# Hybrid decoder layer: 128-byte tiles, query and key norms by 1024 tokens, second half first, memory's part in the middle, state halves swapped by copies

## The chip, the core and the metric

The kernel runs on one core of one Trainium2 chip, as one program. The metric is device microseconds of one execution. Engines are named as the profile names them: PE (TensorE, matmul), DVE (VectorE), ACT (ScalarE), POOL (GpSimd) and SP, whose queue issues all the DMAs here. Each engine runs its own instructions strictly in the order in which the built program holds them.

## The reference

One decoder layer on x of 2048 tokens by 1024 features, all in float32:

```
hn   = rms_norm(x, norm_mix);  proj = hn @ w_in          # q, k, v (512 each), 8 gate logits, u (512)
q, k = rms_norm over each head's 64 columns              # 8 heads
fox  = softmax(q k^T / 8 + c_q - c_k, causal) v          # c = cumsum(log_sigmoid(gate logit))
y    = S5(u): 32 groups of 16 channels, each one complex diagonal state of 64; gelu, then glu
h    = x + [rms_norm(fox), rms_norm(y)] @ w_out
h    = h + cross_attention(rms_norm(h), rms_norm(mem)) @ w_xo     # 256 memory tokens, 4 heads of 256
h    = h + (silu(conv3(gate)) * up) @ w_ffn_down                  # d_ff = 2816
```

Only the first of these stages is touched by the change beyond tile addresses: the input projection, the S5 scan that runs beside it, and the projection of the memory tokens to keys and values.

## The kernel before, in words

Every float32 matmul is made of three (`mm3`, lines 65 to 67), with each operand split into a high and a low part: ACT writes the high part, DVE subtracts it from the source to get the low part (`split`, lines 71 and 72; `split_scaled`, lines 77 and 78, does it with a gain). So each loaded tile costs one pass on ACT and one on DVE.

The stages run one after the other: A (input projection, S5, memory's keys and values), then the causal attention, C (output projection and cross-attention), D and E (the MLP). Stage A ends where the first attention scores (`sps`) begin. It has these parts, in the order of the program:

- The u columns for four chunks of 512 tokens (tile `pps`). Each chunk loads and splits 8 tiles of x and takes the sum of squares of its tokens. When the chunk with c = 2 is on, `mem_norm` (line 289) loads, splits and sums the memory tokens.
- `mem_part` (line 290): 8 blocks of weights for the memory's keys and values (tiles `xkp`, `xvp`). Its first two blocks also reload chunks 0 and 1 of x, because SBUF holds two chunks at a time.
- Twelve units (lines 335 to 361). A unit is one half of the tokens (1024) times one 256-column block of the weights: blocks 0 and 1 are q, 2 and 3 are k, 4 and 5 are v. Each has 192 matmuls of 256 columns. Half 0 comes first, as [2, 0, 1, 3, 4, 5], then half 1 as [4, 0, 2, 1, 3, 5]. Before half 1, `ahead` loads and splits chunks 2 and 3 again, 16 tiles. After the first v block of half 1, `forget` turns the gate logits into the cumulative sums on DVE.

A q or k unit works in four steps of 256 tokens. `qk_begin` (line 307) does 48 matmuls into a PSUM bank (`qps`, four banks in turn), squares it on ACT (`qsq`), sums per head on DVE (`qss`, 8 columns), makes the inverse root with `rinv` (lines 89 to 95: DVE, two ACT instructions, three DVE instructions, all on 8 columns), and multiplies the bank by it on DVE (`qf`). `qk_end` (line 324) comes one step later: PE transposes `qf` (tile `qst`), ACT and DVE split it (`qy`), and two DMAs store it.

The S5 scan is a generator that the stage advances in small steps (`go`, line 229) between its own instructions. After a set-up it handles 16 batches of two groups. For each batch POOL builds rotation tables `er`, `ei` and weights with 12 instructions (`s5_tables`, line 569), and `s5_main` (line 648) does, on a tile whose partitions 0 to 63 hold real parts and 64 to 127 imaginary parts: matmuls to `z`; a rotation, which needs each half multiplied into the other half's place (lines 669 to 672); two scans along time (line 675); a rotation back (lines 681 to 684), of which POOL does one half (line 682); a split; and matmuls to `yp`.

Names that the steps below touch: `et` and `rt` (norms per token), `whl` and `wraw` (weights split and raw), `ul`, `xl`, `tl`, `cl`, `bl` (low parts), `ks`, `bp` (S5 set-up per batch), `gates` and `fsc` (forget).

Of the kernel before, what the change touches and what calls it, by code (L numbers as in the profile page):

```python
# [8 lines left out]
F32 = mybir.dt.float32  # L9
# [14 lines left out]
HD = 64  # L24
# [13 lines left out]
MAGIC = 12582912.0  # L38
TP1 = 6.28125
# [125 lines left out]
def consts(ctx, K, pk):  # L165
# [4 lines left out]
    cp = ctx.enter_context(tc.tile_pool(name="const", bufs=1, reuse_waits="tile"))  # L170
# [37 lines left out]
def stage_a(ctx, K, xT, win, wf, memT, wxk, wxv, qD, kD, vD, uD, cD, xkD, xvD, side):  # L208
# [16 lines left out]
    mp = (tp, wp, xr, xtile, psm, pss)  # L225
# [12 lines left out]
    rp = early.enter_context(tc.tile_pool(name="ar", bufs=1, side="right", reuse_waits="tile"))  # L238
# [33 lines left out]
    for c in range(NC):  # L272
# [19 lines left out]
    def v_unit(half, j, w):  # L292
        for t in range(8 * half, 8 * half + 8):
# [13 lines left out]
    def qk_begin(p, j, w, g, dst):

        ps = psm.tile([128, 2, 256], F32, tag="mm", name="qps")
        for i in range(2):  # L310
            c, o = p // 2, (2 * p + i) % 4 * 128
            for k in range(KT):
                mm3(nc, ps[:, i], x[c][k][0][:, o : o + 128], x[c][k][1][:, o : o + 128], w[0][:, k], w[1][:, k], k == 0, k == KT - 1)
        heads = lambda q: q.rearrange("p i (h d) -> p (i h) d", d=HD)
        sq = tp.tile([128, 2, 256], F32, tag="tm", name="qsq")
        nc.scalar.activation(sq, ps, AF.Square)
        ss = tp.tile([128, 8], F32, tag="ss", name="qss")
        nc.vector.reduce_sum(out=ss, in_=heads(sq), axis=AX.X)
# [3 lines left out]
        return f, p, j, g, dst  # L322

    def qk_end(f, p, j, g, dst):

        st = pss.tile([128, 2, 256], F32, tag="st", name="qst")
        for a in range(2):
            for i in range(2):
                nc.tensor.transpose(st[:, a, i * 128 : (i + 1) * 128], f[:, i, a * 128 : (a + 1) * 128], K.ident)
# [15 lines left out]
    for i, (half, tix) in enumerate(units):  # L345
# [3 lines left out]
        else:  # L349
            for p in range(4 * half, 4 * half + 4):  # L350
                new = qk_begin(p, tix % 2, w, *((K.g_q, qD) if tix < 2 else (K.g_k, kD)))
                if late:
                    qk_end(*late)
# [1476 lines left out]
```

## Time and profile before

| what | value |
|---|---|
| median of 3 runs | 3213.03 us (3209.97 to 3213.67) |
| the profiled execution's own time | 3209.64 us |
| its span, first to last instruction | 3207.7 us |
| mean granted TensorE clock | 0.966 |
| PE busy, share of the span | 94% |
| DVE busy, share of the span | 67% |

The profile describes one execution, whose own time is 1.9 us more than its span. A share of the whole span is a mean over stages that are limited by different things. Stage A takes the first 622 us. "Granted clock" is the mean over a stretch of the TensorE clock, where 1.00 is 2.4 GHz and 0.50 is 1.2 GHz.

### The profile page before, as it was taken

The numbers are of one execution on the slowest core, as the hardware profiler recorded it, in microseconds if no ns is written. First come the engines' busy times: TensorE is split into PE (matmuls) and PEld (weight loads), VectorE is DVE, ScalarE is ACT, GpSimd is POOL, SyncE is SP. The second block draws the span as 40 slices with busy tenths as digits, with TensorE's granted clock in tenths as the row PEclk, the third lists the DMA queues.
The fourth block names the chain that finished last, engine by engine and source line by source line (L and its number), as shares of the span: only waits on it lengthen the run. The fifth ranks groups of instructions, "written<-read, shape, count | busy, mean of one in ns | idle before, by whom it ended". The sixth has DMA issues, their size and how long they took to land.

```text
span 3207.7 us, 43620 instructions
## 1 busy us (share of the span) xinstructions
PE 3012.0 (94%) x15532; PEld 2536.3 (79%) x15532; DVE 2148.2 (67%) x3472; ACT 1451.9 (45%) x2644; POOL 851.9 (27%) x820
## 2 busy tenths in 40 slices
PE   7898978999999899999999697999999999999999
PEld 6687868888888677888878476788788887888887
DVE  8868899688887866444543787777977776443332
ACT  5443333488887634344531343444544444333221
POOL 3615674010000431000000356444444443000000
PEclk9898988999999899999999798999999999999999
DMA  6863434555443663311353335222422222664542
GB/s 194 155 192 107 150 113 127 167 152 151 128 128 114 191 180 128 116 60 63 96 167 126 104 125 179 93 79 86 145 84 81 86 85 103 220 207 157 178 157 84
DMA packets 297649, 421.83 MB, mean 132 GB/s; under 512 B 96341, under 2 KB 168789, under 8 KB 296281
## 3 DMA queue, kind: packets, MB, share of 16 engines
q1 hardware_dynamic: 297432, 419.06, 41.9%
q8 instruction: 122, 2.00, 0.3%
q14 instruction: 95, 0.77, 0.1%
HBM read 304.04 MB, written 114.93 MB: 131 GB/s over the span
## 4 chain that ended last, share of the span: by engine, by line
PE 70%; DVE 12%; DMA 6%; issue 4%; POOL 4%; ACT 3%; SPq 1%; POOLq 0%; DVEq 0%; ACTq 0%
PE da L1567 9%; PE de L1567 6%; PE dps L66 5%; PE dps L67 5%; PE dps L65 5%; PE cmm L65 4%; PE cmm L66 4%; PE cmm L67 4%; PE pt L824 3%; PE dd L1567 3%; PE db L1567 3%; PE sps L790 2%; PE po L817 2%; PE po L818 2%; PE sps L791 2%
## 5 line engine op out<-in xcount | busy, mean ns | idle before, releaser
L1567 PE MATMUL da<-xf,wf 128*128 128x512 f32 x1584 | 380.4, 393 | 19.9 <-ACT xf L71 9.8
L1567 PEld LDWEIGHTS da<-xf,wf 128*128 128x128 f32 x1584 | 299.1, 189 | 86.2 <-ACT xf L71 11.7
L71 ACT CAST whl<-wraw 128x1024 fp32r<-128x1024 f32 (+2 forms) x132 | 155.7, 1203 | 357.8 <-PE dps L67 285.8
L65 PE MATMUL cmm<-act,whl 128*128 128x512 f32 x760 | 308.4, 406 | 2.1 <-DVE h L1220 1.2
L1419 POOL TENSOR_TENSOR wsum<-wraw 128x512 f32<-128x512 f32 x88 | 119.5, 1360 | 717.7 <-DVE h L1391 499.8
L66 PE MATMUL cmm<-act,whl 128*128 128x512 f32 x760 | 302.6, 398 | 3.7 <-DVE act L72 3.7
L67 PE MATMUL cmm<-act,whl 128*128 128x512 f32 x760 | 301.5, 397 | 0.0
L1567 PE MATMUL de<-xf,wf 128*128 128x512 f32 x1056 | 268.9, 405 | 33.2 <-ACT kp L1571 29.1
L65 PE MATMUL dps<-hf,whl 128*128 128x512 f32 x704 | 275.2, 391 | 4.4 <-DVE whl L72 4.4
L66 PE MATMUL dps<-hf,whl 128*128 128x512 f32 x704 | 275.1, 391 | 2.4 <-DVE hf L72 2.4
L67 PE MATMUL dps<-hf,whl 128*128 128x512 f32 x704 | 274.8, 390 | 0.0
L1567 PEld LDWEIGHTS de<-xf,wf 128*128 128x128 f32 x1056 | 206.2, 196 | 83.1 <-ACT kp L1571 32.5
L72 DVE TENSOR_TENSOR whl<-wraw,whl 128x1024 fp32r<-128x1024 f32 (+2 forms) x132 | 190.7, 1466 | 52.2 <-ACT whl L71 51.9
L814 DVE TENSOR_TENSOR pl<-pt,ph 128x512 fp32r<-128x512 f32 (+1 forms) x320 | 186.7, 605 | 22.1 <-ACT ph L828 20.5
L1689 DVE TENSOR_TENSOR res<-dps,res 128x512 f32<-128x512 f32 x32 | 22.1, 691 | 267.0 <-PE dps L67 267.0
L72 DVE TENSOR_TENSOR wf<-wsum,wf 128x512 fp32r<-128x512 f32 x176 | 165.4, 941 | 44.0 <-ACT wf L71 43.5
L66 PEld LDWEIGHTS cmm<-act,whl 128*128 128x128 f32 x760 | 144.9, 191 | 40.6 <-DVE act L72 6.5
L824 PE MATMUL pt<-pk,sb 128*128 128x128 f32 x1088 | 173.1, 276 | 3.9 <-DVE pl L814 2.7
L828 ACT CAST ph<-pt 128x512 fp32r<-128x512 f32 (+1 forms) x320 | 158.9, 521 | 39.0 <-PE pt L824 36.5
L65 PEld LDWEIGHTS cmm<-act,whl 128*128 128x128 f32 x760 | 144.7, 190 | 38.7 <-issue 2.4
L67 PEld LDWEIGHTS cmm<-act,whl 128*128 128x128 f32 x760 | 144.3, 190 | 32.6
L799 ACT ACTIVATE sb<-sb,m 128x128 f32<-128x128 f32 (+15 forms) x128 | 154.6, 1208 | 23.0 <-DVE m L795 22.8
(477 smaller groups left out, 7745.6 us busy)
## 6 DMA issues: line engine op xcount, KB each, us to landing
wraw<-wup SPq DMA_DIRECT2D x88, 512.0 KB
wraw<-wdn SPq DMA_DIRECT2D x64, 704.0 KB
hD<-gt SPq DMA_DIRECT2D x88, 256.0 KB
hraw<-hD SPq DMA_DIRECT2D x88, 256.0 KB
qhl<-qD SPq DMA_DIRECT2D x128, 128.0 KB
wraw<-win SPq DMA_DIRECT2D x28, 512.0 KB
x<-xT SPq DMA_DIRECT2D x32, 256.0 KB
xr<-xT SPq DMA_DIRECT2D x32, 256.0 KB
```

Source lines behind the costliest of these rows:

```text
L65: nc.tensor.matmul(out, lhsT=al, rhs=bh, start=first, stop=False)
L66: nc.tensor.matmul(out, lhsT=ah, rhs=bl, start=False, stop=False)
L67: nc.tensor.matmul(out, lhsT=ah, rhs=bh, start=False, stop=last)
L71: nc.scalar.copy(hi, src)
L72: (eng or nc.vector).tensor_tensor(lo, src, hi.bitcast(F32), op=ALU.subtract)
L790: nc.tensor.matmul(out, lhsT=ql[:, o : o + 128], rhs=kc, start=True, stop=False)
L799: nc.scalar.activation(sb[:, :wid], sb[:, :wid], AF.Exp, bias=m, scale=-1.0, accum_out=self.ls[:, i : i + 1])
L814: v.tensor_tensor(b, c, a.bitcast(F32), op=ALU.subtract)
L824: nc.tensor.transpose(ps[:, j * 128 : (j + 1) * 128], rows[j][:, kt * 128 : (kt + 1) * 128], K.ident)
L828: nc.scalar.copy(ph[:, s], ps[:, s])
L1419: gp.tensor_tensor(t, x, y, op=op)
L1567: nc.tensor.matmul(ps, lhsT=w[:, a, k], rhs=x[k][:, b], start=first and k + j == 0, stop=k == 3 and j == 2, skip_group_check=not first)
```

## The change

- All SBUF pools go through `Rounded`, which pads a tile's free size to a multiple of 128 bytes, and a 96-byte tile at the right edge moves the pools there to such multiples. The eight gain columns become slices of one tile `gains`.
- The memory's part (`mem_norm`, `mem_part`) moves from ahead of the twelve units to between the sixth and the seventh.
- The units of half 1 come first. Chunks 2 and 3 are still in SBUF then, so their reload goes; chunks 0 and 1 are reloaded in `mem_part` as before.
- A q or k unit copies each step's PSUM bank to SBUF on ACT (`qf`, 8 buffers in a pool of their own). The sums of squares of all four steps go into one tile of 32 columns, `norms` makes one `rinv` for them, in the next unit, and multiplies the four `qf` tiles in place. The transposes (`end`) follow after that.
- In `s5_main`, ACT copies the two halves of `z` and of the scan's result `w3` crosswise into a tile `cross`, and the rotations become DVE instructions on all 128 partitions. POOL's half of the rotation back goes to DVE. Signs move from one sum to the other.

```diff
+class Rounded:
+    def tile(self, shape, dtype, **kw):
+        unit = 64 if dtype == BF16 else 32
+        n = math.prod(shape[1:])
+        if n % unit == 0:
+            return self.pool.tile(shape, dtype, **kw)
+        t = self.pool.tile([shape[0], -(-n // unit) * unit], dtype, **kw)[:, :n]
...
-        if c + 2 == NC:
-            mem = mem_norm(K, mp, memT)
-    mem_part(K, mp, mem, wxk, wxv, xkD, xvD, lambda c: load(c, xr, "xr", 4), go)
...
-        r = rinv(K, tp, ss, 8, 1.0 / HD, et[:, 2 * p : 2 * p + 2].rearrange("p i h -> p (i h)"), tag="rsm")
-        f = tp.tile([128, 2, 256], F32, tag="qf", name="qf", bufs=3)
-        nc.vector.tensor_tensor(heads(f), heads(ps), r.unsqueeze(2).broadcast_to([128, 8, HD]), op=ALU.mult)
...
+        def begin(self, n):
...
+            f = fp.tile([128, 2, 256], F32, tag="qf", name="qf")
+            nc.scalar.copy(f, ps)
+            sq = tp.tile([128, 2, 256], F32, tag="tm", name="qsq")
+            nc.scalar.activation(sq, ps, AF.Square)
+            nc.vector.reduce_sum(out=self.ss[:, n], in_=sq.rearrange("p i (h d) -> p (i h) d", d=HD), axis=AX.X)
+            self.f.append(f)
+
+        def norms(self):
+            e = et[:, 8 * self.half : 8 * self.half + 8].rearrange("p i h -> p (i h)")
+            r = rinv(K, tp, self.ss.rearrange("p n h -> p (n h)"), 32, 1.0 / HD, e, tag="rsm")
+            for n, f in enumerate(self.f):
+                q = f.rearrange("p i (h d) -> p (i h) d", d=HD)
+                nc.vector.tensor_tensor(q, q, r[:, 8 * n : 8 * n + 8].unsqueeze(2).broadcast_to([128, 8, HD]), op=ALU.mult)
...
-    units = [(half, tix) for half in range(2) for tix in ([4,0,2,1,3,5] if half else [2,0,1,3,4,5])]
-
-    def ahead(i):
-        if i == 6:
-            for c in (2 * units[i][0], 2 * units[i][0] + 1):
-                load(c, xr, "xr", 4)
-        return weights(units[i][1])
...
+    units = [(half, tix) for half in (1, 0) for tix in ([4, 0, 2, 1, 3, 5] if half == 0 else [2, 0, 1, 3, 4, 5])]
...
+        if i == 5:
+            mem = mem_norm(K, mp, memT)
...
+            new = QK(half, tix % 2, w, *((K.g_q, qD) if tix < 2 else (K.g_k, kD)))
+            for n in range(4):
+                new.begin(n)
+                if n == 0 and late:
+                    late.norms()
+                if n > 0:
+                    end(n - 1)
                 go(1.3)
...
+        if i == 5:
+            mem_part(K, mp, mem, wxk, wxv, xkD, xvD, lambda c: load(c, xr, "xr", 4), go)
...
+    def crossed(src):
+        t = sp.tile([128, n, 256], F32, tag="cr", name="cross")
+        nc.scalar.copy(t[0:64], src[64:128])
+        nc.scalar.copy(t[64:128], src[0:64])
+        return t
+
+    zc = crossed(z)
     v.tensor_tensor(w1, z, er, op=ALU.mult)
-    v.tensor_tensor(w2[0:64], z[64:128], ei[64:128], op=ALU.mult)
-    v.tensor_tensor(w2[64:128], z[0:64], ei[0:64], op=ALU.mult)
-    v.tensor_tensor(w1, w1, w2, op=ALU.add)
+    v.tensor_tensor(w2, zc, ei, op=ALU.mult)
+    v.tensor_tensor(w1, w1, w2, op=ALU.subtract)
...
-    gp.tensor_tensor(x2[0:64, :, a], w3[64:128, :, p], ei[64:128, :, p], op=ALU.mult)
-    v.tensor_tensor(x2[64:128, :, a], w3[0:64, :, p], ei[0:64, :, p], op=ALU.mult)
-    v.tensor_tensor(x1[:, :, a], x1[:, :, a], x2[:, :, a], op=ALU.subtract)
+    v.tensor_tensor(x2[:, :, a], wc[:, :, p], ei[:, :, p], op=ALU.mult)
+    v.tensor_tensor(x1[:, :, a], x1[:, :, a], x2[:, :, a], op=ALU.add)
```

The built program's order shows the change at three places. Line numbers of before and of the change differ for the same text: `rinv` is at L89 to L95 before and at L115 to L121 now, `split` at L71 and L72 before and at L97 and L98 now.

On DVE, one step of the first k unit before (`qss` is the sum of squares per head, `rs_v` the inverse root, `qf` the normed tile):

```order
L318 TENSOR_REDUCE qss<-qsq 128x8
L89 SCALAR_TENSOR_TENSOR rs_v<-qss,et 128x8
L93 TENSOR_TENSOR rs_v<-rs_v,rs_y 128x8
L94 TENSOR_TENSOR rs_v<-rs_v,rs_y 128x8
L95 SCALAR_TENSOR_TENSOR rs_v<-rs_v,rs_y 128x8
L321 TENSOR_TENSOR qf<-qps,rs_v 128x512
```

On DVE, the whole first k unit now:

```order
L357 TENSOR_REDUCE qss<-qsq 128x8 x4
L115 SCALAR_TENSOR_TENSOR rs_v<-qss,et 128x32
L98 TENSOR_TENSOR whl<-wraw,whl 128x1024 x2
L119 TENSOR_TENSOR rs_v<-rs_v,rs_y 128x32
L120 TENSOR_TENSOR rs_v<-rs_v,rs_y 128x32
L121 SCALAR_TENSOR_TENSOR rs_v<-rs_v,rs_y 128x32
L365 TENSOR_TENSOR qf<-qf,rs_v 128x512 x4
```

Four chains of four small instructions on 8 columns have become one on 32 columns, and the multiplication reads `qf` in SBUF instead of `qps` in PSUM.

On DVE, the rotations of one S5 batch before (`w` and `x` are its work tiles, `z` is in PSUM; L675 is the scan):

```order
L669 TENSOR_TENSOR w_2882<-z,er 128x512
L321 TENSOR_TENSOR qf<-qps,rs_v 128x512
L670 TENSOR_TENSOR w_2883<-z,ei 64x512
L671 TENSOR_TENSOR w_2883<-z,ei 64x512
L672 TENSOR_TENSOR w_2882<-w_2882,w_2883 128x512
L675 SCALAR_TENSOR_TENSOR w_2969<-s_rho,w_2882 128x256 x2
L72 TENSOR_TENSOR tl<-tr,th 128x256
L681 TENSOR_TENSOR x_2972<-w_2969,er 128x2x255
L683 TENSOR_TENSOR x_2973<-w_2969,ei 64x2x255
```

On DVE, the rotations of the second S5 batch now:

```order
L735 TENSOR_TENSOR w_2539<-z,er 128x512
L736 TENSOR_TENSOR w_2540<-cross,ei 128x512
L737 TENSOR_TENSOR w_2539<-w_2539,w_2540 128x512
L740 SCALAR_TENSOR_TENSOR w_2554<-s_rho,w_2539 128x256 x2
L747 TENSOR_TENSOR x_2560<-w_2554,er 128x2x255
L748 TENSOR_TENSOR x_2561<-cross,ei 128x2x255
L684 TENSOR_TENSOR ks<-kp,s_dd 128x32
L749 TENSOR_TENSOR x_2560<-x_2560,x_2561 128x2x255
```

Two half-width instructions on `z` have become one that reads ACT's copy, and each reader of `cross` stands directly behind one other DVE instruction.

On ACT, a stretch of a q unit before (`qsq` is the square, `qy` the split of the transposed tile, `rs_y` the two logarithm and exponential instructions of `rinv`):

```order
L316 ACTIVATE qsq<-qps 128x512
L77 ACTIVATE qy<-qst,sg_q 128x512
L91 ACTIVATE rs_y<-rs_v 128x8
L92 ACTIVATE rs_y<-rs_y 128x8
L71 CAST xh<-x_2726 128x512
```

On ACT, a stretch of a q unit now, with the first S5 batch in it:

```order
L729 COPY cross<-z 64x512
L730 COPY cross<-z 64x512
L729 COPY cross<-w_2298 64x512
L730 COPY cross<-w_2298 64x512
L354 COPY qf<-qps 128x512
L356 ACTIVATE qsq<-qps 128x512
L103 ACTIVATE qy<-qst,gains 128x512
L97 CAST xh<-x_2304 128x512
```

ACT now stands between `z` and DVE's rotation, and again between the scan and the rotation back; the copy and the square of the next `qps` bank are queued behind both pairs.

## Rows read from the trace of the kernel before

**Rows 1.** The page's first part: busy time, share and instructions of each engine.

```profile
PE 3012.0 (94%) x15532; PEld 2536.3 (79%) x15532; DVE 2148.2 (67%) x3472; ACT 1451.9 (45%) x2644; POOL 851.9 (27%) x820
```

**Rows 2.** Stretches of stage A: length; PE, PEld, DVE, ACT, POOL busy; clock; DMA share; GB/s.

```profile
0.00:135.00 135.00, 106.62 (x430) 85.15 (x430) 117.52 (x265) 65.16 (x116) 69.42 (x151) 0.91 0.74 171
135.00:196.00 61.00, 54.37 (x395) 52.14 (x396) 40.01 (x56) 30.26 (x54) 10.41 (x10) 0.93 0.71 217
196.00:568.00 372.00, 313.52 (x2382) 306.54 (x2382) 320.87 (x508) 127.10 (x278) 210.09 (x198) 0.91 0.42 128
568.00:598.00 30.00, 29.44 (x246) 29.09 (x246) 21.39 (x44) 10.84 (x25) 2.10 (x4) 1.00 0.37 115
598.00:622.00 24.00, 23.35 (x196) 23.12 (x194) 6.45 (x15) 5.43 (x12) 0.00 (x0) 1.00 0.69 225
```

**Rows 3.** What PE waited for, 196 to 622 us: total, times, longest.

```profile
PE qst L329 <- DVE qf L321: 29.3, 12, 6.4
PE yp L65 <- DVE ks L628: 8.8, 2, 7.7
PE z L66 <- DVE ul L72: 7.5, 4, 5.6
PE yp L66 <- DVE xl L72: 6.4, 3, 3.6
```

**Rows 4.** DVE's groups by shape, 196 to 598 us: busy, mean ns | idle before.

```profile
L683 DVE TENSOR_TENSOR x<-w,ei 64x510 f32<-64x510 f32 x16 | 22.8, 1425 | 0.5
L321 DVE TENSOR_TENSOR qf<-qps,rs_v 128x512 f32<-128x512 f32 x31 | 21.2, 685 | 0.6
...
L78 DVE SCALAR_TENSOR_TENSOR xl<-xr,sg_mix,xh 128x512 fp32r<-128x512 f32 x20 | 18.5, 968 | 0.4 <-ACT xh L77 0.3
L72 DVE TENSOR_TENSOR xl<-x,xh 128x512 fp32r<-128x512 f32 x16 | 15.9, 993 | 0.2
...
L94 DVE TENSOR_TENSOR rs_v<-rs_v,rs_y 128x8 f32<-128x8 f32 x31 | 13.8, 446 | 0.5
L93 DVE TENSOR_TENSOR rs_v<-rs_v,rs_y 128x8 f32<-128x8 f32 x31 | 13.7, 443 | 2.9 <-ACT rs_y L92 2.9
L89 DVE SCALAR_TENSOR_TENSOR rs_v<-qss,et 128x8 f32<-128x8 f32 x31 | 13.0, 418 | 0.1
...
L670 DVE TENSOR_TENSOR w<-z,ei 64x512 f32<-64x512 f32 x16 | 11.1, 693 | 0.3
...
L95 DVE SCALAR_TENSOR_TENSOR rs_v<-rs_v,rs_y 128x8 f32<-128x8 f32 x31 | 11.0, 355 | 0.5
L671 DVE TENSOR_TENSOR w<-z,ei 64x512 f32<-64x512 f32 x16 | 10.9, 684 | 0.3
```

**Rows 5.** DVE's timeline in the last unit, where POOL is idle: start, us.

```profile
599.28 0.15 DVE L89 SCALAR_TENSOR_TENSOR rs_v<-qss,et 128x8 f32<-128x8 f32 x1
599.95 0.17 DVE L93 TENSOR_TENSOR rs_v<-rs_v,rs_y 128x8 f32<-128x8 f32 x1 [0.52 <-ACT rs_y L92]
```

**Rows 6.** ACT's groups, 196 to 598 us: a copy from PSUM, one from SBUF.

```profile
L695 ACT COPY yt<-yp 128x512 f32<-128x512 f32 x16 | 9.3, 580 | 3.8 <-PE yp L67 2.0 <-issue 1.8
L71 ACT CAST uh<-ur 128x512 fp32r<-128x512 f32 x15 | 9.3, 618 | 8.0 <-PE yp L67 7.9
```

**Rows 7.** POOL's half of the rotation back, 196 to 598 us.

```profile
L682 POOL TENSOR_TENSOR x<-w,ei 64x510 f32<-64x510 f32 x16 | 25.7, 1608 | 1.1
```

**Rows 8.** DVE's groups, 1300 to 1800 us (stage C): the split of `hl`.

```profile
L72 DVE TENSOR_TENSOR act<-hl,act 128x512 fp32r<-128x512 f32 x32 | 21.5, 689 | 13.6 <-ACT act L71 13.1
```

**Rows 9.** DVE's groups, 2800 to 3208 us (stage E): the split of `hraw`.

```profile
L72 DVE TENSOR_TENSOR hf<-hraw,hf 128x512 fp32r<-128x512 f32 x60 | 38.6, 688 | 16.2 <-ACT hf L71 16.1
```

**Rows 10.** Two stretches without POOL, stages C and E; columns as in Rows 2.

```profile
1400.00:1600.00 200.00, 200.00 (x1090) 170.59 (x1089) 100.48 (x248) 95.89 (x229) 0.00 (x0) 1.00 0.21 70
3000.00:3208.00 208.00, 203.71 (x899) 168.36 (x897) 57.62 (x54) 40.74 (x40) 0.00 (x0) 0.99 0.37 124
```

More of the change, by code (lines that the diff above doesn't have):

```diff
@@ L60, with __init__, pool_of @@
     pass
+class Rounded:
+    def __init__(self, pool):
+        self.pool = pool
+    def tile(self, shape, dtype, **kw):
[4 more added lines that the diff above has]
+        t = self.pool.tile([shape[0], -(-n // unit) * unit], dtype, **kw)[:, :n]
+        if len(shape) == 2:
+            return t
+        names = "abcd"[: len(shape) - 1]
+        return t.rearrange(f"p ({' '.join(names)}) -> p {' '.join(names)}", **dict(zip(names, shape[1:])))
+@contextmanager
+def pool_of(tc, **kw):
+    with tc.tile_pool(**kw) as p:
+        yield p if "space" in kw else Rounded(p)
 def mm3(nc, out, ah, al, bh, bl, first, last):
@@ L303, in v_unit @@
             nc.sync.dma_start(vD[rows(t), 4 * j : 4 * j + 4], s.bitcast(F32))
+            end(t - 8 * half - 2)
             if t % 2:
                 go(1.2)
[L307 to L318, printed above, removed]
-        r = rinv(K, tp, ss, 8, 1.0 / HD, et[:, 2 * p : 2 * p + 2].rearrange("p i h -> p (i h)"), tag="rsm")
-        f = tp.tile([128, 2, 256], F32, tag="qf", name="qf", bufs=3)
-        nc.vector.tensor_tensor(heads(f), heads(ps), r.unsqueeze(2).broadcast_to([128, 8, HD]), op=ALU.mult)
-        return f, p, j, g, dst
@@ L345, in stage_a, with end @@
+    units = [(half, tix) for half in (1, 0) for tix in ([4, 0, 2, 1, 3, 5] if half == 0 else [2, 0, 1, 3, 4, 5])]
+    late = None
+    def end(n):
+        nonlocal late
+        if late and 0 <= n < 4:
+            late.end(n)
+            if n == 3:
+                late = None
+    nxt = weights(units[0][1])
     for i, (half, tix) in enumerate(units):
         w = nxt
+        if i + 1 < len(units) and i != 5:
+            nxt = weights(units[i + 1][1])
+        if i == 5:
+            mem = mem_norm(K, mp, memT)
@@ L347, in stage_a @@
         if tix in (4, 5):
-            v_unit(half, tix - 4, w)
-        else:
[L350 to L353, printed above, removed]
-                late = new
-                go(1.3)
-        if i + 1 < len(units):
-            nxt = ahead(i + 1)
-        if i == 6 + [4,0,2,1,3,5].index(4):
+            if late:
+                late.norms()
+            v_unit(half, tix - 4, w, end)
+        else:
+            new = QK(half, tix % 2, w, *((K.g_q, qD) if tix < 2 else (K.g_k, kD)))
+            for n in range(4):
+                new.begin(n)
+                if n == 0 and late:
+                    late.norms()
+                if n > 0:
+                    end(n - 1)
+                go(1.3)
+            end(3)
+            late = new
@@ L359, in stage_a @@
+        if i == 5:
+            mem_part(K, mp, mem, wxk, wxv, xkD, xvD, lambda c: load(c, xr, "xr", 4), go)
+            nxt = weights(units[i + 1][1])
+        if i == 6:
             forget(K, lambda: xr.tile([128, 512], F32, tag="xr", name="fsc"), pss, gates, cD)
@@ L420, in s5_setup @@
     o = PK["s_b"][0]
-    with tc.tile_pool(name="s5t", bufs=1, side="right", reuse_waits="tile") as sp:
+    with pool_of(tc, name="s5t", bufs=1, side="right", reuse_waits="tile") as sp:
         w = lambda n, s=sh: sp.tile(s, F32, name="s5t_" + n)
```

99 lines of the change are left out of this document (59 added, 40 removed).

## The prediction

> **What bounds the kernel now.** I read the page's busy times first, then stage A in stretches, then PE's waits there, then DVE's groups. Over the whole span PE is busy 94% and DVE 67% [rows 1], and that would say that DVE's work costs nothing. Stage A says something else. From 196 to 568 us, which holds units one to ten less a little, DVE is busy 320.87 of 372 us (86%), PE only 313.52, and the clock is 0.91 [rows 2]. In the last unit, where S5 is over, 192 matmuls take 24 us at clock 1.00 with DVE busy 6.45 [rows 2]. So PE itself needs far less than the 372 us: it idles 372 - 313.5 = 58.5 us, and a mean clock of 0.91 between the levels 1.00 and 0.50 means 0.18 of the time, 67 us, at half speed, whose work would take half as long. That is another 33.5. PE's own floor for the stretch is 372 - 58.5 - 33.5 = 280 us. What it waits for is DVE: the transposes for `qf` 29.3 us, S5's matmuls for `ks`, `ul` and `xl` 22.7 [rows 3]. The four largest waits all name it. I therefore count DVE's time from 196 to 598 us as the price, and PE's 92 us as the most that can come back there.
>
> Why DVE is so full shows in its small instructions. A step of `rinv` on 8 columns takes 0.15 and 0.17 us in the last unit, while POOL is idle [rows 5], but 418, 443, 446 and 355 ns on average where POOL is busy 210 of 372 us [rows 2, 4]. The subtraction on 128x512 takes 993 where 688 is the time without POOL [rows 4, 9]. These instructions are held up by POOL's, several tenths of a microsecond at a time, whatever their own size.
>
> **The change part by part.**
>
> *Norms by 1024 tokens.* 32 chains of `rinv` become 8. A chain costs 418 + 443 + 446 + 355 = 1662 ns on DVE [rows 4]; 32 of them 53.2 us, less 1.0 because one stands in the last unit at 0.66. The trace has no chain on 32 columns. From below it is the 0.15 + 3 x 0.17 = 0.66 us of the free chain, so 5.3 for 8; from above the held-up 1.66, so 13.3, since 24 more columns add little next to what the waits are. I take 13.3, POOL being as busy as before: **39 us saved** (39 to 47). ACT loses 48 small instructions, off the path.
>
> The multiplication into `qf` now reads SBUF twice instead of PSUM and SBUF. Before, it took 685 with no delay beside the same POOL work [rows 4]. From below it costs what it did; from above what the subtraction with two SBUF inputs takes, 993, that is 32 x 0.31 = 9.9 us more. I take half, **5 us lost**. The Trainium skill has a rule that speaks against this edit: SBUF — State Buffer, section "Who interferes with whom", says that a DVE instruction with two SBUF inputs contends with a GpSimd instruction that reads SBUF, by an exclusive lock, and one with a single SBUF input does not. The rows agree (685 beside 993), and by the rule this term stands nearer 10 than 0, which would make the sum 46 instead of 51. The same rule is why the `rinv` rows are long.
>
> The copy of `qps` on ACT is 32 x 0.58 = 18.6 us [rows 6]. ACT is busy 127 of 372 us [rows 2], so it is hidden there; it is not free if ACT's queue stands, which is a rival below. In return the transposes come a full unit's norms later, and the 29.3 us wait for `qf` loses its cause.
>
> *Second half first.* 16 loads of 256 KB go, with 16 splits: 16 x 0.968 = **15.5 us saved on DVE** [rows 4] and as many on ACT.
>
> *Memory's part between.* It moves work and removes none. Its 61 us have DVE busy at 40 and PE at 54 [rows 2]; S5's set-up steps that went with it move to the first units, and the main steps of S5 move into it. DVE's sum is the same, and the first units, like the memory part before, leave it slack. I take 0, with 10 us either way: up, the waits for the first memory weights may vanish; down, its splits now meet POOL's tables.
>
> *State halves by copies.* Removed per batch: 693 + 684 + 1425 ns [rows 4], 16 times, 44.8 us. Added: two full-width instructions with two SBUF inputs, between 688 [rows 9] and 993 ns [rows 4] each, 32 in all: 22.0 to 31.8; the middle is 27. **18 us saved** (13 to 23). POOL loses 25.7 us [rows 7], which can only shorten the hold-ups.
>
> *What the copies make DVE wait.* The order shows `w<-z,er` directly ahead of `w<-cross,ei`, and `x` directly ahead of `x<-cross,ei`. ACT needs 2 x 0.58 to 0.62 = 1.2 us for a pair [rows 6], the DVE instruction in between hides about 0.7, so DVE stands 0.5 us, 32 times: **16 us lost**. Behind it in DVE's queue are the sums and splits that feed the next `qst`, `z` and `yp`. Nothing is lost where another instruction stands between; where ACT is still in a 0.6 us instruction, it is 1.1 us each, 35 in all.
>
> *Tiles at multiples of 128 bytes.* In the built program `hl` lies at such a multiple and `hraw` 96 bytes past one; DVE's split takes 689 and 688 [rows 8, 9]. The DMAs show no difference either: 70 GB/s at a share of 0.21 is 333 GB/s at full share, 124 at 0.37 is 335 [rows 10]. Taken at 0. Behind the first attention scores the order of every engine soon is the one of before, so nothing else moves.
>
> **The sum.** 39 - 5 + 15.5 + 18 - 16 = 51 us of DVE's time, in a stretch that DVE sets, and below the 92 that PE could give back. Bounds of the terms: 39 - 9.9 + 15.5 + 13 - 35 = 23 and 47 + 15.5 + 23 = 85; with the memory part's 10, 13 to 95. The profiled execution's 3209.64 us less 51 is 3158.6; the median of the runs is 3.4 above that execution, so I predict **3162 us**, 3128 to 3190 if this mechanism holds.
>
> **The rivals.**
>
> *PE becomes the bound.* If the waits for DVE vanish altogether, the 58.5 us of idling and the 33.5 of half clock come back: 3213 - 92 = 3121. For it: every large wait names DVE [rows 3]. Against it: DVE after the change still has about 320.87 + 21.39 - 67 = 275 us, and 16 more of waiting, beside 280 for PE, and two engines so nearly equal, each in order, do not overlap without gaps.
>
> *The handoffs eat the gain.* ACT serves `cross` late each time: the 35 us bound, with `qf` at its upper bound too, leaves 23, and a memory part that gets 10 worse leaves 13: 3200.
>
> *Slower, by ACT's queue.* In ACT's order the second pair of copies stands directly behind the first, and waits for DVE's rotation and two scans, some 3 us, with the copy and square of the next `qps` bank behind it. PE has four banks of 24 / 4 = 6 us of matmuls each, so it stops only if ACT is late by two banks, 12 us, beyond the one in work and the one being read. If DVE's backlog does that in each batch, PE and DVE lose 3 + 1.2 us in 16 batches, 67 us against the 51: 3229. Against it: ACT has been busy a third of the stretch, and 12 us is four times the chain that it would wait for.
>
> *No change in effect.* The waits for `qf` go but the same time appears as waits for `xl` and `ul`, because S5's chain of matmul, rotation, scan, rotation and matmul is what paces the steps: within 6 us of 3213.
>
> **How the numbers follow.** Forecast (gain 23 to 85 us) 0.66; PE bound (85 to 100) 0.12; handoffs (6.4 to 23) 0.10; no change 0.05; slower 0.07. 0.2% is 6.4 us, about what a measurement of this kernel can tell from no change. Faster is 0.66 + 0.12 + 0.10 = 0.88, same 0.05, slower 0.07. The range of 3118 to 3202 takes in the bounds of the terms and the middle of the PE case, and leaves out some 0.2: the last two cases, and the ends of the others.
>
> **What would show it.** In the profile after: stage A ends near 571 us instead of 622; the `rinv` rows are 8 per line at 0.2 to 0.5 us; the wait for `qf` has shrunk below 5 us; `qf` takes 0.7 to 1.0; the rows that read `cross` show an idle time of about 0.5 us each with ACT as the releaser; the clock of the units is above 0.95; the stages behind keep their length. I am wrong if DVE's idle time ahead of `cross` is over 1 us each, if ACT's copy of `qps` shows PE as waiting for it, or if any stage behind the first scores changes by more than a few us.

## The result, and the profile after

The change is faster by 0.9%: 3181.11 us, the median of 4 runs (3179.26 to 3186.98), against 3211.5 us of before (4 runs). The ratio is 0.9912, with a 95% interval of 0.9897 to 0.9926, so some 28 us. The forecast was 3162 us, in a range of 3118 to 3202: the direction and the range held, and little more than half of the 51 us came. Stage lengths and busy times below are those of one profiled execution of each kernel (3209.64 us before, 3181.56 changed), so differences of a few microseconds in them are no finding by themselves.

Where it came from is read first from stretches. Before, cut at the end of the first projections and at the first attention scores (columns as in [rows 2]):

```profile
0.00:130.30 130.30, 106.62 (x430) 85.15 (x430) 112.82 (x261) 65.16 (x116) 64.72 (x147) 0.91 0.76 175
130.30:621.90 491.60, 420.59 (x3211) 410.79 (x3211) 393.42 (x627) 173.54 (x367) 227.29 (x216) 0.92 0.46 142
```

The changed kernel, cut at the same places:

```profile
0.00:138.50 138.50, 106.53 (x426) 84.98 (x427) 105.90 (x240) 55.02 (x92) 68.36 (x154) 0.89 0.66 151
138.50:602.30 463.80, 412.58 (x3217) 403.23 (x3215) 349.90 (x520) 218.65 (x423) 201.76 (x193) 0.94 0.47 145
```

Stage A ends 19.6 us earlier, not 51. The first projections got 8.2 us longer; the rest of the stage (units and memory's part) got 27.8 us shorter, although DVE, which was to set its pace, is busy 43.5 us less there. Of the 27.8 us, 8.0 are PE's own busy time, for the same matmuls at a clock of 0.94 instead of 0.92, and 19.8 its idle time. The other 8 us of the gain lie in stage C. Its matmuls give that to the tenth (tile view of `cmm`: duration min/median/max, first and last start, form). Before:

```profile
L67 PE MATMUL cmm<-act,whl x760: 388/394/628, 1105.6 to 1791.6; 128*128 128x512 f32 x190
L65 PE MATMUL cmm<-act,sb x8: 395/397/792, 1079.7 to 1101.6; 128*128 128x512 f32 x8
```

After:

```profile
L93 PE MATMUL cmm<-act,whl x760: 387/389/628, 1087.3 to 1765.0; 128*128 128x512 f32 x190
L91 PE MATMUL cmm<-act,sb x8: 388/394/796, 1061.1 to 1083.0; 128*128 128x512 f32 x8
```

From the first of them to the last it is 1791.6 - 1079.7 = 711.9 us before and 1765.0 - 1061.1 = 703.9 us now, and the median matmul went from 394 to 389 ns.

What PE waits for in the changed units, which answers to [rows 3]:

```profile
PE z L92 <- DVE ul L98: 9.5, 5, 6.0
PE z L91 <- ACT uh L97: 9.3, 7, 4.4
PE yp L91 <- DVE ks L684: 8.4, 4, 3.6
PE xvp L92 <- DVE whl L98: 7.7, 3, 5.9
PE ist L175 <- DVE nacc L155: 5.8, 1, 5.8
```

The 29.3 us for `qf` are gone from the list. DVE's groups there, which answer to [rows 4]:

```profile
L365 DVE TENSOR_TENSOR qf<-qf,rs_v 128x512 f32<-128x512 f32 x32 | 21.4, 716 | 0.2
L749 DVE TENSOR_TENSOR x<-x,x 128x510 f32<-128x510 f32 x16 | 21.1, 1321 | 0.2
L98 DVE TENSOR_TENSOR xl<-x,xh 128x512 fp32r<-128x512 f32 x16 | 18.5, 1153 | 2.6 <-ACT xh L97 2.6
...
L748 DVE TENSOR_TENSOR x<-cross,ei 128x510 f32<-128x510 f32 x16 | 16.2, 1011 | 4.9 <-ACT cross L730 4.8
...
L736 DVE TENSOR_TENSOR w<-cross,ei 128x512 f32<-128x512 f32 x16 | 11.5, 722 | 0.0
...
L735 DVE TENSOR_TENSOR w<-z,er 128x512 f32<-128x512 f32 x16 | 11.0, 686 | 11.3 <-ACT cross L730 11.1
...
L115 DVE SCALAR_TENSOR_TENSOR rs_v<-qss,et 128x32 f32<-128x32 f32 x8 | 3.8, 471 | 0.0
```

And DVE's waits for `cross` there (total, times, longest):

```profile
DVE w L735 <- ACT cross L730: 11.1, 7, 3.0
DVE x L748 <- ACT cross L730: 4.8, 6, 1.7
```

Most single terms look as forecast: a chain of `rinv` starts with 471 ns and there are 8 of them, `qf` takes 716, and the two readers of `cross` take 11.5 + 16.2 = 27.7 us (27 forecast). DVE stands 11.1 + 4.8 = 15.9 us for `cross` (16 forecast), but this agrees in the sum alone: not each of the 32 pairs waits 0.5 us, but 13 of them, 1.2 us on average and up to 3.0. The idle time of the first rotation stands at the row of `w<-z,er` because the wait is put ahead of the pair. And `xl<-x,xh`, which the change does not touch, went from 993 [rows 4] to 1153 ns. Over the whole stage DVE is busy 112.8 + 393.4 = 506.2 us before and 105.9 + 349.9 = 455.8 now, 50.4 less; the forecast's terms without the waits, 39 - 5 + 15.5 + 18, make 67. So part of DVE's saving came back in other rows, and the stage gave less than half of what was left.

### The profile page after: what moved, and what is told of

The parts are those of the page before. It is cut to its first block, busy times and chain, and to the rows that moved or that the text cites. A ratio compares the mean times of both kernels' runs of the same rounds, so it can differ in the third digit from the quotient of the medians.

```text
span 3179.8 us, 43457 instructions
## 1 busy us (share of the span) xinstructions
PE 2993.7 (94%) x15532; PEld 2526.4 (79%) x15532; DVE 2095.4 (66%) x3344; ACT 1485.6 (47%) x2676; POOL 832.6 (26%) x804
## 4 chain that ended last, share of the span: by engine, by line
PE 72%; DVE 12%; issue 4%; DMA 4%; ACT 3%; POOL 3%; SPq 0%; DVEq 0%; POOLq 0%; ACTq 0%
PE da L1632 9%; PE de L1632 6%; PE dps L92 5%; PE dps L93 5%; PE dps L91 5%; PE cmm L91 4%; PE cmm L92 4%; PE cmm L93 4%; PE pt L889 3%; PE dd L1632 3%; PE db L1632 3%; PE po L882 2%; PE po L883 2%; PE sps L855 2%; PE sps L856 1%
## 5 line engine op out<-in xcount | busy, mean ns | idle before, releaser
L1632 PEld LDWEIGHTS da<-xf,wf 128*128 128x128 f32 x1584 | 298.7, 189 | 84.5 <-ACT xf L97 10.8
L97 ACT CAST whl<-wraw 128x1024 fp32r<-128x1024 f32 (+2 forms) x132 | 155.2, 1206 | 343.9 <-PE dps L93 288.0
L91 PE MATMUL cmm<-act,whl 128*128 128x512 f32 x760 | 304.7, 401 | 4.0 <-DVE h L1285 2.6
L92 PE MATMUL cmm<-act,whl 128*128 128x512 f32 x760 | 299.0, 393 | 4.4 <-DVE act L98 4.4
L93 PE MATMUL cmm<-act,whl 128*128 128x512 f32 x760 | 297.9, 392 | 0.0
L98 DVE TENSOR_TENSOR whl<-wraw,whl 128x1024 fp32r<-128x1024 f32 (+2 forms) x132 | 193.9, 1495 | 31.1 <-ACT whl L97 30.0
L879 DVE TENSOR_TENSOR pl<-pt,ph 128x512 fp32r<-128x512 f32 (+1 forms) x320 | 186.8, 605 | 21.7 <-ACT ph L893 19.6
L98 DVE TENSOR_TENSOR wf<-wsum,wf 128x512 fp32r<-128x512 f32 x176 | 164.8, 938 | 44.0 <-ACT wf L97 43.5
```

The lines of the kernel that those rows point to most:

```text
L91: nc.tensor.matmul(out, lhsT=al, rhs=bh, start=first, stop=False)
L92: nc.tensor.matmul(out, lhsT=ah, rhs=bl, start=False, stop=False)
L93: nc.tensor.matmul(out, lhsT=ah, rhs=bh, start=False, stop=last)
L97: nc.scalar.copy(hi, src)
L98: (eng or nc.vector).tensor_tensor(lo, src, hi.bitcast(F32), op=ALU.subtract)
L879: v.tensor_tensor(b, c, a.bitcast(F32), op=ALU.subtract)
```

## The experiments

Each was timed beside runs of the kernel before on its own chip (their medians are 3206.8 to 3211.5 us), so kernels are compared by their ratios. "Units" is the stretch from the end of the first projections to the first scores, with memory's part in it, and the busy times are those of that stretch in the profiled execution.

| kernel | median us | ratio to before (95%) | projections end | units, us | PE | DVE | POOL |
|---|---|---|---|---|---|---|---|
| before | 3211.5 | 1 | 130.3 | 491.6 | 420.6 | 393.4 | 227.3 |
| changed | 3181.11 | 0.9912 (0.9897 to 0.9926) | 138.5 | 463.8 | 412.6 | 349.9 | 201.8 |
| align_only | 3200.83 | 0.9980 (0.9972 to 0.9989) | 130.5 | 491.2 | 418.5 | 393.3 | 226.5 |
| no_align | 3186.65 | 0.9938 (0.9926 to 0.9951) | 136.5 | 463.4 | 411.5 | 350.9 | 200.3 |
| cross_old | 3201.99 | 0.9979 (0.9970 to 0.9988) | 137.5 | 482.5 | 418.7 | 378.3 | 224.8 |
| order_old | 3184.44 | 0.9924 (0.9911 to 0.9936) | 130.2 | 471.5 | 414.8 | 351.2 | 203.3 |
| norms_only | 3200.03 | 0.9970 (0.9958 to 0.9982) | 129.8 | 486.2 | 419.1 | 378.0 | 232.1 |
| copies_only | 3183.69 | 0.9917 (0.9901 to 0.9934) | 130.9 | 469.9 | 411.2 | 365.7 | 203.7 |
| z_copies | 3202.23 | 0.9982 (0.9972 to 0.9993) | 129.9 | 490.0 | 418.9 | 384.2 | 227.0 |
| w3_copies | 3180.73 | 0.9910 (0.9895 to 0.9925) | 131.6 | 470.3 | 411.4 | 377.6 | 199.3 |
| tables_once | 3132.55 | 0.9759 (0.9741 to 0.9777) | 137.2 | 412.5 | 393.5 | 284.3 | 10.9 |
| late_setup | 3189.38 | 0.9939 (0.9921 to 0.9958) | 119.4 | 489.5 | 414.4 | 352.2 | 220.4 |
| uh2 | 3184.88 | 0.9924 (0.9908 to 0.9941) | 137.7 | 468.5 | 408.6 | 347.0 | 197.6 |
| uh2_old | 3178.72 | 0.9905 (0.9887 to 0.9922) | 129.9 | 469.0 | 410.4 | 345.6 | 197.9 |

**Alignment alone, and all but alignment.** align_only is the kernel before with `Rounded`, the edge tile and `gains`, all instructions in their old order; no_align takes these out of the changed kernel:

```diff
-        unit = 64 if dtype == BF16 else 32
-        n = math.prod(shape[1:])
-        if n % unit == 0:
+        if True:
             return self.pool.tile(shape, dtype, **kw)
```

> The kernel before with one part of the change alone: every tile at a multiple of 128 bytes, the order of all instructions as before. Theory (TensorE reads a moving operand faster from such a multiple): about 8 us faster than before, nearly all of it in stage C (from about 1070 to 2000 us), where the 128x512 matmuls that read act follow each other every 227 ns throughout instead of 234 in half of the passes; stage A's end moves by less than 3 us. Rival (the prediction on record: alignment is worth 0, and stage C gained by waits that the other parts of the change took away): within 3 us of before, 234 ns stay or no time follows from them.

> The changed kernel with its tiles packed as before, the order of its instructions kept. Theory: about 8 us slower than the changed kernel, so some 20 us faster than before; cmm from act at 234 ns in the passes over misaligned tiles. Rival: the same time as the changed kernel, some 28 us faster than before.

The theory held in both, by direction and by the medians' ratios. The units are the same (491.2 for 491.6, 463.4 for 463.8), and in stage C the first and last matmul lie 703.9 us apart in align_only:

```profile
L93 PE MATMUL cmm<-act,whl x760: 387/389/632, 1106.1 to 1783.7; 128*128 128x512 f32 x190
L91 PE MATMUL cmm<-act,sb x8: 388/394/797, 1079.8 to 1102.5; 128*128 128x512 f32 x8
```

and 1771.6 - 1059.3 = 712.3 us apart in no_align. The trace of before held the cause within itself: the last pass of stage C goes chunk by chunk, and in the built program its `act` tiles, the moving operand of these matmuls (the one that is streamed past the loaded weights), start 32 or 96 bytes past a multiple of 128 in the even chunks, and at one in the odd; the weights (`whl`) start at one throughout. Two stretches of it in the kernel before, an odd chunk and then an even one, both without a wait:

```profile
1660.00:1698.00 38.00, 38.00 (x167) 31.13 (x166) 16.13 (x25) 10.26 (x18) 0.00 (x0) 1.00 0.49 154
1705.00:1742.00 37.00, 37.00 (x158) 29.49 (x157) 10.38 (x15) 5.06 (x8) 0.00 (x0) 1.00 0.27 93
```

and the same time in align_only, where that chunk runs 7 to 8 us earlier (the last 2.7 us belong to the next one):

```profile
1705.00:1742.00 37.00, 37.00 (x163) 30.37 (x162) 10.17 (x15) 4.43 (x7) 0.00 (x0) 1.00 0.33 109
```

38.00 / 167 is 227.5 ns from one matmul to the next, 37.00 / 158 is 234.2, and 37.00 / 163 is 227.0. From the first to the last of its 192 matmuls the even chunk takes 45.5 us before and 44.5 in align_only, and the odd one ahead of it 44.2 in both (starts of the matmuls in the traces). PE streams a 128x512 operand 7 ns slower from such an address, and nothing hides it there.

The 8.0 us are not all of this kind. In z_copies, described below, all tiles are aligned and the median matmul takes 389 ns too:

```profile
L93 PE MATMUL cmm<-act,whl x760: 387/389/632, 1104.7 to 1791.6; 128*128 128x512 f32 x190
L91 PE MATMUL cmm<-act,sb x8: 388/395/795, 1078.5 to 1101.3; 128*128 128x512 f32 x8
```

Yet the stage took 1791.6 - 1078.5 = 713.1 us in its profiled execution, and 709.0 and 709.6 in those of order_old and copies_only, at a mean clock of 0.97 to 0.98. By the trace's clock records, PE had the lower of its two clock levels for 30.1 us of stage C before, 23.0 in align_only, 33.3 in copies_only, 36.6 in order_old and 40.2 in z_copies. With that time counted at half, stage C takes 695.4 and 696.9 us in the two kernels with packed tiles and 690.1 to 693.3 in the twelve with aligned ones. So some 4 us of stage C are shown for the addresses; the rest of the 8.0 is a difference of the clock, which changes from one kernel's profiled execution to another's without the addresses. By the ratio of all its runs, align_only gains 6.4 us, with an interval of 3.5 to 9.0.

**The copies undone, and the order undone.** cross_old has the old rotations of `s5_main` in the changed kernel, order_old the old order of the stage:

```diff
-    units = [(half, tix) for half in (1, 0) for tix in ([4, 0, 2, 1, 3, 5] if half == 0 else [2, 0, 1, 3, 4, 5])]
+    units = [(half, tix) for half in (0, 1) for tix in ([4, 0, 2, 1, 3, 5] if half == 1 else [2, 0, 1, 3, 4, 5])]
...
+        if c + 2 == NC:
+            mem = mem_norm(K, mp, memT)
+    mem_part(K, mp, mem, wxk, wxv, xkD, xvD, lambda c: load(c, xr, "xr", 4), go)
```

> The changed kernel with the rotations of S5's states as before (two half-height instructions each, one of them on GpSimd, no copies by ScalarE). By the terms on record (18 saved on VectorE, 16 lost to waits for cross) about 2 us slower than the changed kernel, 5 either way. Rival 1 (ScalarE's queue stands for the copies and makes qsq and th late, which eats what the norms gave back): 8 or more us faster than the changed kernel, VectorE's wait for qsq back from 35 to about 13 us. Rival 2 (the copies carry the gain, since GpSimd's long instruction is what held VectorE up): 10 to 20 us slower.

> The changed kernel with the first stage in the order of before: memory's part behind the first projections, then the first half, then the second, with 16 more loads and splits. By the terms on record it is 15.5 us slower than the changed kernel, with 10 either way. Rival 1 (memory's part between the halves costs what the 16 loads give, since its stretch took 78.6 us in the changed kernel and 65.2 before, and the first projections took 8 us more): within 5 us of the changed kernel. Rival 2 (the new order is a loss): faster than the changed kernel by 5 to 15 us.

cross_old lost 21 us: rival 2 (10 to 20), far from the 2 us of the terms on record. With the old rotations, norms and order together move the end of stage A only from 621.9 to 137.5 + 482.5 = 620.0 us. order_old is within 4 us of the changed kernel, and the intervals overlap: rival 1. Its stage A ends at 130.2 + 471.5 = 601.7, the changed one's at 602.3. DVE is busy 114.2 + 351.2 = 465.4 us in the whole stage of order_old and 455.8 in the changed kernel: the dropped reload is worth 9.6 us of DVE, not 15.5, and nothing of the stage's end. The new order makes the units 7.7 us shorter and the first projections 8.3 longer. In the changed kernel PE stands there once for long (PE's timeline):

```profile
54.15 0.39 PE L91 MATMUL pps<-xh,whl 128*128 128x512 f32 x1
67.68 2.08 PE L175 MATMUL ist<-nacc,pk 128*128 128x512 f32 x2 [13.13 <-DVE nacc L155]
```

In order_old the longest such wait is 9.0 us. All waits for `nacc` in the first projections make 13.5 us there and 17.7 here, and here 3.9 for `usb` come with them: together the 8. DVE's timeline just before shows what was ahead of the sums of squares in its queue, S5's set-up, itself waiting for POOL:

```profile
56.59 0.46 DVE L608 TENSOR_SCALAR s5t_c<-s5t_bc 128x512 f32<-128x512 f32 x1 [1.89 <-POOL s5t_cq L527]
...
58.69 0.79 DVE L155 TENSOR_TENSOR nacc<-nsq 128x512 f32<-128x512 f32 x1
```

**Norms alone, copies alone, no tables, and the set-up moved back.** The first two stand on align_only. tables_once and late_setup are edits of the changed kernel; tables_once leaves out 14 of the 16 table computations, so its result is another:

```diff
-            t[b + 2] = s5_tables(K, S, sp, b + 2)
+            t[b + 2] = kept[b % 2] = s5_tables(K, S, sp, b + 2) if b < 0 else kept[b % 2]
```

```diff
                 if c > 0:
-                    go(1.5)
+                    with tc.issue_after(K.sums.ins):
+                        go(1.5)
```

> The kernel before with aligned tiles and the norms by 1024 tokens, in the old order of the stage and with the old rotations; to be held against align_only (6.4 us faster than before). Theory 1 (what paces the units is S5's batch, from z to yp and back to uh, one after the other; small VectorE instructions elsewhere fit beside it): within 6 us of align_only, though VectorE is busy some 35 us less. Theory 2 (the terms on record: VectorE's busy time paces the units, norms are worth 34): some 30 us faster than align_only.

> The kernel before with aligned tiles and ScalarE's copies of the state halves alone, norms and order as before; to be held against align_only. Theory 1: 12 to 20 us faster than align_only, since the rotations lie inside S5's batch. Theory 2 (the terms on record, 18 saved less 16 of waits): about 2 us faster than align_only.

> The changed kernel with S5's tables computed on GpSimd for the first two batches alone and used again by the other fourteen: it leaves out 14 of 16 table computations, so its output is another. If GpSimd's instructions hold VectorE's up, the rows of x, xl, ul, tl, cl and whl fall to what they take without GpSimd (0.68, 0.69, 0.68, 0.42, 0.42 and 1.22 us), some 2 us a batch and 14 in the splits, and stage A ends 25 to 40 us earlier. Rival (the hold-ups lie where VectorE has slack): the rows fall, and stage A ends less than 8 us earlier.

> The changed kernel with VectorE's set-up for S5 queued behind the sums of squares of the chunk it was written after, as the queue stood before. If the order of that queue is what made the first projections 8 us longer, they end near 130 us instead of 138 and the kernel is 5 to 8 us faster than the changed one. Rival (the set-up is then late for the first batch, and S5's batches set the end): the first projections end near 130, and the end of stage A moves by less than 3 us.

norms_only is 5.0 us shorter in the units than align_only, at 15.3 us less of DVE: theory 1 by its number, and not a gain beyond the noise (ratios 0.9970 and 0.9980, with overlapping intervals). copies_only is 21.3 us shorter, which refutes theory 2; with the copies in place the norms add nothing (order_old 471.5, copies_only 469.9). Where the norms' saving went shows in the groups of two kernels. DVE in align_only, and then in norms_only:

```profile
L713 DVE TENSOR_TENSOR x<-x,x 128x510 f32<-128x510 f32 x16 | 15.6, 974 | 0.2
L98 DVE TENSOR_TENSOR xl<-x,xh 128x512 fp32r<-128x512 f32 x16 | 15.5, 968 | 0.2
L119 DVE TENSOR_TENSOR rs_v<-rs_v,rs_y 128x8 f32<-128x8 f32 x32 | 14.4, 451 | 3.4 <-ACT rs_y L118 3.4
```

```profile
L367 DVE TENSOR_TENSOR qf<-qf,rs_v 128x512 f32<-128x512 f32 x32 | 24.5, 810 | 0.2
...
L741 DVE TENSOR_TENSOR x<-x,x 128x510 f32<-128x510 f32 x16 | 20.5, 1279 | 1.2 <-POOL x L739 0.6
L98 DVE TENSOR_TENSOR xl<-x,xh 128x512 fp32r<-128x512 f32 x16 | 19.4, 1212 | 1.7 <-ACT xh L97 1.7
...
L119 DVE TENSOR_TENSOR rs_v<-rs_v,rs_y 128x32 f32<-128x32 f32 x8 | 5.2, 654 | 0.7 <-ACT rs_y L118 0.6
```

All `rinv` rows on 8 or 32 columns together fell from 53.6 to 13.6 us, 40.0 saved where the forecast had 39. But `x<-x,x` rose by 305 ns and `xl` by 244, 16 times each, so 8.8 us came back in two groups that do the same work as before; `qf`, which now has two inputs in SBUF, took 810 ns instead of 685 [rows 4], 2.6 us more of busy time in its 32 rows (24.5, and 21.9 in align_only). POOL is as busy as it was (232.1 and 226.5 us). The hold-ups had not belonged to the small instructions; what stands there next takes them over. PE's waits in the units of norms_only, beside [rows 3]:

```profile
PE yp L91 <- DVE ks L684: 20.5, 7, 7.6
PE z L92 <- DVE ul L98: 15.5, 8, 7.0
PE yp L92 <- DVE xl L98: 7.0, 4, 3.6
```

The wait for `qf` went, and the waits for `ks`, `ul` and `xl` grew from 22.7 to 43.0 us. At the longest wait for `ul`, PE's timeline and then DVE's:

```profile
342.64 0.58 PE L92 MATMUL z<-ul,bh 128*128 128x256 f32 x1 [7.03 <-DVE ul L98]
```

```profile
336.75 4.84 DVE L367 TENSOR_TENSOR qf<-qf,rs_v 128x512 f32<-128x512 f32 x4
341.52 0.47 DVE L104 SCALAR_TENSOR_TENSOR vs<-vps,rt,vs 128x256 fp32r<-128x256 f32 x1
341.91 0.67 DVE L98 TENSOR_TENSOR ul<-ur,uh 128x512 fp32r<-128x512 f32 x1
```

A unit's four multiplications now come in one piece, and here 4.84 us of them stood ahead of the split that PE was waiting for.

tables_once shows how large the hold-ups are. Its units, and three of DVE's groups in them:

```profile
137.20:549.70 412.50, 393.49 (x3218) 387.01 (x3216) 284.33 (x520) 217.21 (x423) 10.94 (x25) 1.00 0.51 158
```

```profile
L98 DVE TENSOR_TENSOR whl<-wraw,whl 128x1024 fp32r<-128x1024 f32 x34 | 40.9, 1218 | 9.9 <-ACT whl L97 9.7
...
L98 DVE TENSOR_TENSOR xl<-x,xh 128x512 fp32r<-128x512 f32 x16 | 11.0, 685 | 2.9 <-ACT xh L97 2.9
L749 DVE TENSOR_TENSOR x<-x,x 128x510 f32<-128x510 f32 x16 | 11.0, 684 | 0.2
```

Every row fell to its length without POOL, as expected, and the units got 51.3 us shorter, more than the 40 that was expected at most; DVE is busy 65.6 us less and the mean clock of its units is 1.00. POOL's results do not come late in either kernel: in the units of both, the one wait for them is ACT's for `wxc` (10.7 us in the changed kernel, 10.8 here). The Trainium skill, in SBUF — State Buffer, section "Who interferes with whom", says that a DVE instruction with two SBUF inputs contends with a POOL instruction that reads SBUF, by an exclusive lock, and that one with a single SBUF input does not. These rows agree: `x<-x,x` goes from 1321 to 684 ns, while `w<-z,er`, which reads PSUM and SBUF, takes 686 beside POOL and 691 here.

late_setup shows that the 8 us of the first projections are not there for the taking. They end at 119.4, 19 us earlier than in the changed kernel, and the stage ends at 119.4 + 489.5 = 608.9, 6.6 us later, which neither the expectation nor its rival had. PE's waits right behind them (119 to 200 us), and those of SP's queue from 100 to 152 us:

```profile
PE qst L374 <- DVE qf L366: 11.9, 1, 11.9
PE qps L91 <- ACT whl L97: 8.6, 1, 8.6
```

```profile
SPq L611 <- POOL s5t_far L529: 15.2, 1, 15.2
SPq L611 <- POOL s5t_gbr L529: 11.5, 1, 11.5
```

SP's stores of the set-up's results (`parD`) wait for it longer now, and the next unit's weights are queued behind them: ACT waited 16.83 us for `wraw` there. The first matmul of S5's first batch started at 211.3 us, 6.5 later than in the changed kernel.

**Which of the two copies, and a second buffer.** On align_only, z_copies has the copies for the rotation of `z` alone, w3_copies those for the rotation back, which takes POOL's half away:

```diff
-    gp.tensor_tensor(x2[0:64, :, a], w3[64:128, :, p], ei[64:128, :, p], op=ALU.mult)
-    v.tensor_tensor(x2[64:128, :, a], w3[0:64, :, p], ei[0:64, :, p], op=ALU.mult)
-    v.tensor_tensor(x1[:, :, a], x1[:, :, a], x2[:, :, a], op=ALU.subtract)
+    v.tensor_tensor(x2[:, :, a], wc[:, :, p], ei[:, :, p], op=ALU.mult)
+    v.tensor_tensor(x1[:, :, a], x1[:, :, a], x2[:, :, a], op=ALU.add)
```

uh2 and uh2_old give `uh` and `ul` two buffers, in the changed kernel and in order_old; for the room `ur` loses its second buffer and `yt` shares that of `w3`, so they loosen one wait and may tighten another:

```diff
-    uh = sp.tile([128, n, 256], F32R, tag="uh", name="uh")
-    ul = sp.tile([128, n, 256], F32R, tag="ul", name="ul")
+    uh = sp.tile([128, n, 256], F32R, tag="uh", name="uh", bufs=2)
+    ul = sp.tile([128, n, 256], F32R, tag="ul", name="ul", bufs=2)
```

> align_only with ScalarE's copies for the first rotation alone (z, ahead of the scans); the second rotation keeps GpSimd's half. To be held against align_only (8 us faster than before at its median) and copies_only (26). Theory 1 (what counts is the time inside S5's batch: with both pairs of copies, the piece from the first product to the first scan fell from 4.2 to 2.6 us a batch and the piece from the scans to the last sum stayed at 3.7): 14 to 20 us faster than align_only. Rival (what counts is that GpSimd's 1.6 us instruction is gone): less than 5 us faster than align_only.

> The other half: align_only with the copies for the second rotation alone (w3, behind the scans), so that GpSimd's half is gone and the first rotation keeps its two half-height instructions. Theory 1: within 5 us of align_only. Rival (GpSimd's relief): 12 to 18 us faster than align_only.

> The changed kernel with two buffers for uh and ul, so that the next batch's split need not wait until TensorE has read the last one in yp; ur has one buffer and yt shares w3's for the room. Theory 1 (the batches pace the units, and each waits at z for uh and ul, 18.8 us in all): 8 to 19 us faster than the changed kernel, and the waits of z for uh and ul below 5 us. Rival (the wait moves on to ks, xl or the next bank): within 4 us of the changed kernel.

> The same two buffers on order_old, the changed kernel with the stage in its old order, where z waits 24.8 us for uh and ul: by theory 1 10 to 24 us faster than order_old, and so the fastest of the kernels that compute all, at some 3160 to 3172 us. Rival as for uh2: within 4 us of order_old.

Here theory 1 fell. z_copies shortened its piece of the batch as foreseen (from the first product to the first scan 2.8 us on average, worked out from the starts of the rows, instead of 4.2) and took 9.1 us off DVE, but gained only 1.2 us in the units and, by its ratio, nothing (0.9982, and 0.9980 of align_only). w3_copies gained 20.9 us in the units and has the ratio of the changed kernel (0.9910 and 0.9912), with the old norms, the old order and half of the copies. Its stretch:

```profile
131.60:601.90 470.30, 411.43 (x3213) 401.56 (x3212) 377.58 (x627) 192.77 (x399) 199.28 (x199) 0.95 0.49 149
```

What it took away is POOL's 27 us, and with them 7 us in DVE's own rotation row (22.7 in align_only, 15.6 as `x<-cross,ei`) and 11 us in the `rinv` rows that it did not touch (53.6 to 42.5); `x<-x,x` and `xl` rose by 199 and 117 ns. A shorter chain on DVE within the batch was not the gain: from the first product to the end of the split of `x` a batch takes 13.3 us in align_only and in w3_copies, and 12.2 in z_copies, which gained nothing (means of 16, worked out from starts and ends of the rows). In uh2 the waits of `z` did leave the list, and others took their place, as its rival said:

```profile
PE yp L91 <- DVE ks L684: 12.7, 6, 4.6
PE foff L459 <- DVE fsc L457: 10.3, 1, 10.3
```

Its units are 4.7 us longer than the changed kernel's. uh2_old is 2.5 us shorter there than order_old, and 6 us faster by its ratio, with overlapping intervals. Neither kernel is better than the changed one beyond its interval.

## Why the prediction was half right

The direction, what PE waited for and most of DVE's single rows were read rightly. That the time lies in the range is luck in good part. Of the 51 us, 39 - 5 + 15.5 = 49.5 stood for the norms and the reload, which show no gain beyond the noise. What came is the alignment, which stood at 0, and the second pair of copies, which stood at 18 - 16 = 2 together with the first: w3_copies has only these two and gains as much as the whole change.

The step that failed is the one behind the first part, "I therefore count DVE's time from 196 to 598 us as the price": a microsecond of DVE was taken for a microsecond of the stage. Term by term:

| term | forecast | DVE busy, measured | units and stage, measured |
|---|---|---|---|
| norms, with `qf` | 39 - 5 | 15.3 less (`rinv` 40.0 less, `qf` 2.6 more, the rest back in other rows) | 5.0 alone (within the noise), nothing beside the copies |
| rotations by copies | 18 - 16 | 27.6 less; 15.9 of waits for `cross` in the changed kernel | 21.3 together; alone, 1.2 for `z` and 20.9 for `w3` |
| reload dropped, memory between | 15.5 + 0 | 9.6 less over the whole stage | 7.7 in the units, 8.3 lost in the first projections |
| alignment | 0 | 0 | 8.0 in stage C, some 4 of it by the addresses |

*Norms.* The instruction count and the durations of the `rinv` rows came as priced; that the held-up time is POOL's was in the text as "several tenths of a microsecond at a time, whatever their own size", and that it would then move to the next instruction was not drawn from it. What was left of the gain became idle time of DVE, as PE waited for S5's operands instead of `qf`. That is the mechanism of the rival "No change in effect", given 0.05; it held for this part of the change, and only as a shift of waits, since shortening S5's own batch (z_copies) or loosening it (uh2, with the buffers that it cost) did not help either.

*Copies.* Their direct cost and the sum of their waits were right, 27 and 16 us, though the waits came as fewer and longer ones than forecast. Mis-sized is the clause that POOL's loss of 25.7 us "can only shorten the hold-ups", which stood at 0 in the sum: the edit that takes this work off POOL, and makes DVE's half-height row a full one, is worth 20.9 by itself, with DVE 15.7 us less busy. Since 15.3 us less of DVE in norms_only and 9.1 in z_copies brought 5.0 and 1.2, POOL's share is the likely cause, but no run has it alone. ACT's queue, the rival on the other side, did stand (`qss` waited 35.5 us for `qsq`, 12.7 before, over the units), and cost less than this gave.

*The reload.* The saving is there in part (9.6 us of DVE); the forecast left out that the new order puts S5's set-up ahead of a chunk's sums in DVE's queue. late_setup shows that moving it back costs more than it gives.

*Alignment.* The check was made on a DVE split and a DMA rate, and PE's operands were not looked at, although the trace of before holds both cases in one pass. That "the stages behind keep their length" did not hold: stage C became 8.0 us shorter, and a change of more than a few us behind the first scores was a sign named for being wrong.

Of the other signs, the stage's end (602 instead of 571) and the clock (0.94 instead of over 0.95) were wrong, the 8 rows of `rinv` and `qf` at 0.7 right. The half microsecond ahead of each reader of `cross` is right as a mean alone: six of the 32 pairs wait over 1 us, the limit named for being wrong, and 19 hardly wait. PE did not become the bound: the clock stays below 1.00 and the waits remain; it comes near that only in tables_once, where PE is busy 393.5 of 412.5 us.

Open is why POOL's half of the rotation is worth 0.77 us of the stage for each of its 27 us, while the tables are worth 51.3 / 190.9 = 0.27 for each of theirs. It runs beside the DVE instruction that computes the other half, in the middle of a batch, and the tables run anywhere; that is an argument and no measurement. Its half on DVE without any copy was not tried, nor were smaller bursts of norms.

## What to carry to other kernels

When short VectorE instructions are slow beside a busy GpSimd, ask whose time it is. Here it was that of GpSimd's instructions: removing the short ones handed much of it to the next, and moving 27 us of GpSimd's work away brought more than 40 us of saved VectorE rows. A busy share, even of 86%, does not price a microsecond: look for what PE will wait for once the named wait is gone, and price that. And compare a matmul's cadence (the time from one start to the next) on the same shape from tiles at different addresses before taking their alignment for nothing.

## What the runs showed of the hardware that was not expected

- PE takes 234 ns from one 128x512 float32 matmul to the next when the moving tile starts 32 or 96 bytes past a multiple of 128, and 227 from a multiple (clock 1.00). Whether a smaller multiple would do is not shown. DVE's split showed no difference at 96 bytes [rows 8, 9].
- With 14 of 16 table computations off POOL, every DVE row with two SBUF inputs fell to the length it has beside an idle POOL, in S5's batches by up to 637 ns (`x<-x,x` 1321 to 684).
